# Attention scores over all 128 rows of the array, and the sample's score and sum tiles of four heads in a row

## The chip, the cores and the metric

The kernel runs on one core of a Trainium2 chip. TensorE (PE) multiplies, VectorE (DVE), ScalarE (ACT) and GpSimd (POOL) do the elementwise work, SyncE (SP) issues most of the DMAs. Each engine works through its own list of instructions in order and waits on semaphores for the others. The metric is the device time of one launch in microseconds (us); lower is better.

## The reference

One layer of a streaming encoder, for a prompt of 512 tokens and a sample of 32 tokens that continues a cache of 512. Two branches start from one projection: RWKV-7 time mixing, and differential attention, of which the change touches only the second. Cut to that:

```python
def diff_attend(q, k, v, lam, mask):          # 8 heads, two maps c of 64 dims per head, v of 128 dims
    s = jnp.einsum('bqhcd,bkhcd->bchqk', q, k) * (DA_HEAD_DIM ** -0.5)
    if mask is not None:                       # prompt: block causal, chunks of 64
        s = jnp.where(mask, s, -1e30)
    p = jax.nn.softmax(s, axis=-1)
    pd = p[:, 0] - lam * p[:, 1]
    return jnp.einsum('bhqk,bkhd->bqhd', pd, v)
# sample: keys and values are the 512 cached rows and the 32 new ones, no mask
```

The result is normalised per head and projected (w_o_da), gated together with the other branch, projected again, and goes through a gated feed-forward layer. All of it is float32.

## The kernel before, in words

**Precision.** Most matrix products are done in the format fp32r: every operand is kept as a high part and a low part, and a product is the sum of high x high, high x low and low x high. `dense` (L139 is its matmul) does this for all projections, on weight tiles that `load_w` loads (L119, SP), rounds on ACT (L120) and subtracts on DVE or POOL (L121). The attention's transposes, probability x value products and everything of the sample's attention are plain float32; the trace shows two records for each such matmul.

**Stages.** First the RWKV projections and recurrence (to about 690 us), then the attention of eight heads (690 to 912 us), then merge, output projection, feed-forward and final norm. Under the attention run the *fillers*: the projections of v and of the branch gates that are left over, and the RWKV output projection. They are recorded with a low priority (`tc.high_priority(offset=LOW)`), and a scheduler that plans with its own durations places every engine's instructions: where the attention has nothing ready by its plan, it puts matmuls of L139. The order on each engine is then fixed.

**A head of the prompt** (loop over `h`, L997 on). DMAs of L1008 bring q and k of each map m twice, the 64 dims once on partitions `hi` (the map's own half) and once on `lo` (the other half): `rQ`, `rK`. ACT rounds them to `xQ`, `xK` (L1010). For q, DVE overwrites the `lo` half of `xQ` with the low parts, so `xQ` is [high; low] on 128 rows. For k, `xK` stays high parts on both halves, and the low parts go to the map's half of one tile `KL` (L1012). For each block of 128 queries i and map m, PE does two matmuls into the PSUM tile `sc`:

```python
PE.matmul(sc[m][:, 0:n], Q[m][:, qb], KH[m][:, 0:n], start=True, stop=False)      # L1031: 128 rows
PE.matmul(sc[m][:, 0:n], Q[m][f, qb], KL[f, 0:n], start=False, stop=True)         # L1032: 64 rows
```

DVE takes the row maximum, ACT the exponentials, DVE combines both maps (`pd`), PE transposes `pd` (L1045), ACT copies it (`pdt`), PE multiplies by `vtok` (L1049). Every one of these tiles has few buffers; `rK`, `xK` and `KL` have one.

**The sample** (`attend_sample`, called after heads 3 and 7 for four heads each). For each head e, a DMA brings its 256 KB of cached keys into the one buffer `kc` (L938), and PE does two score matmuls of 64 rows and 32 columns, one a map (L940), at `tile_position=(64 * m, 32 * e)`. L946 does the same for the new keys. After the softmax come, for each head e, a 256 KB DMA of cached values into `vtok` (L987), four matmuls of 128 rows and 32 columns (L989) and one of 32 rows and 32 columns for the new values (L991), at `tile_position=(0, 32 * e)`.

Of the kernel before, what the change touches and what calls it, by code (L numbers as in the profile page):

```python
# [10 lines left out]
F32 = mybir.dt.float32  # L11
F32R = mybir.dt.float32r
# [10 lines left out]
# tiles whose weights are split on GpSimd (projections of the recurrence, as (pair, which)) and on  # L23
# VectorE (the other projections, the recurrence's output projection from 40 on)
# [6 lines left out]
PAST = 512  # L31
# [34 lines left out]
def tile_hybrid_layer(  # L66
# [57 lines left out]
    def dense(src, total, xh, xl, evac, le=None, whole=None):  # L124
        """src: weight tile in DRAM of total row blocks; evac(psum, c0, c1) for both column halves.
        whole: pool that holds all of the tile's weights, for one column half after the other."""
        ps = [psd[0].tile([128, 272], F32, name="psd") for _ in HALVES]
        parts = [(b, min(WK, total - b)) for b in range(0, total, WK)]
        ws = {}
        both = range(len(HALVES))  # L130
        for hf, (base, kt) in ([(h, p) for h in both for p in parts] if whole else [(h, p) for p in parts for h in both]):
            if base not in ws:
                ws[base] = load_w(src[:, base * 128:(base + kt) * 128], kt, le or V, whole or wpool)
            wh, wl = ws[base]
            c0, c1 = HALVES[hf]
            for k in range(kt):
                kk = base + k
                for ip, (w, x) in enumerate(((wh, xh), (wh, xl), (wl, xh))):
                    PE.matmul(ps[hf][:, :c1 - c0], w[:, k, :], x[:, kk, c0:c1],  # L139
                              start=(kk == 0 and ip == 0), stop=(kk == total - 1 and ip == 2))  # L140
            if base + kt == total:
                evac(ps[hf][:, :c1 - c0], c0, c1)
# [5 lines left out]
    def newton_wide(y, x, t):  # L148
        """y ~ x**-0.5, one Newton step, all SBUF"""
        A.activation(out=t, in_=y, func=AF.Square)  # L150
        V.scalar_tensor_tensor(out=t, in0=t, scalar=-0.5, in1=x, op0=ALU.mult, op1=ALU.mult)
        V.scalar_tensor_tensor(out=y, in0=t, scalar=1.5, in1=y, op0=ALU.add, op1=ALU.mult)

    def rsqrt_tiny(pool, x, n, tag):
        """x**-0.5 for a [p, n] tile of positive numbers"""
        p = x.shape[0]
        yt = pool.tile([128, 16], F32, name=tag + "y", bufs=2)
        tt = pool.tile([128, 16], F32, name=tag + "t", bufs=2)
        y, t = yt[:p, :n], tt[:p, :n]
        V.tensor_scalar(out=y.bitcast(I32), in0=x.bitcast(I32), scalar1=-0.5, scalar2=1597463007.0,  # L160
                        op0=ALU.mult, op1=ALU.add)
        for _ in range(4):
            V.tensor_tensor(out=t, in0=y, in1=y, op=ALU.mult)
            V.scalar_tensor_tensor(out=t, in0=t, scalar=-0.5, in1=x, op0=ALU.mult, op1=ALU.mult)
            V.scalar_tensor_tensor(out=y, in0=t, scalar=1.5, in1=y, op0=ALU.add, op1=ALU.mult)
        return y
# [6 lines left out]
    def rms_scale(x, t, rs, ss, c0, c1):  # L173
        """rs[:, c0:c1] <- (ss / 1024 + eps)**-0.5 for the sums of squares ss in PSUM; x, t: scratch"""
# [56 lines left out]
    def shifted(idx, out, rs=None):  # L231
        """evacuation of a projection and the token shift after it; rs: the columns' scale where it is still to come"""
# [32 lines left out]
    # the array's clock rises while the first operands are on their way  # L265
# [45 lines left out]
    # [high; low] parts of both low-rank inputs, for weights held twice  # L311
# [31 lines left out]
    # ================= phase 1: RWKV, q and k projections =================  # L343
# [10 lines left out]
    # persistent work tiles  # L354
# [15 lines left out]
    def diag16(flat):  # L370
        """the two diagonal 16x16 blocks of a 32x32 matrix kept in rows of 32"""
# [5 lines left out]
    def inverse(npf):  # L377
        """diagonal 16-blocks of Xp <- transposed inverses of (I - N) of the strictly lower blocks N of npf"""
# [11 lines left out]
    def rw_rates(p):  # L390
        """decay and in-context rate of a pair's channels"""
# [13 lines left out]
        # decay: tanh of the low-rank product, cumulated in chunks  # L405
# [10 lines left out]
        # in-context rate  # L416
# [4 lines left out]
    def rw_elem(p, Pt, Pi, ta, kr, r, vv):  # L421
# [3 lines left out]
        def head_sum(t, names, use):  # L425
            """use(psum, c0, c1) of t's sums over each head"""
# [9 lines left out]
        # normalised key  # L436
# [16 lines left out]
        # kmod and bonus  # L453
# [11 lines left out]
        # A~ R~ B~ K~, the sample's chunk behind the others  # L465
# [7 lines left out]
        # rows (K; B) of a chunk's products for the even head, (B; K) for the odd one  # L473
# [14 lines left out]
    def chunk_products(dst, m0, a, b):  # L488
        """masked products of a pair's chunks: rows (K; B) for the even head, (B; K) for the odd one"""
# [13 lines left out]
    def join16(rows, src, M, xt):  # L503
        """xt (block diagonal of transposed 16-inverses) <- transposed 32-inverses; src(q, m): transposed N"""
# [23 lines left out]
    def rw_super(s):  # L528
# [3 lines left out]
        # inverses of the 16-blocks of every chunk, then of the 32-blocks, then the block below them  # L532
        # (even heads have their rows at partitions 64.., odd heads at 0..)
# [38 lines left out]
    def rw_chain(p0, ms):  # L572
# [19 lines left out]
        # chain over the chunks  # L592
# [52 lines left out]
    def rw_norm(p0, ysb):  # L645
        """group norm over the head's values, bonus, gate"""
# [28 lines left out]
    def by_dims(d):  # L675
        """rows of all heads' maps as [map, dim, token]; a tile of a projection holds 8 dims of every map"""
        return d.rearrange("a (m d) t -> (a m) d t", m=2)
# [137 lines left out]
    # rotary on the staged rotated halves  # L815
# [38 lines left out]
    # ================= attention =================  # L854
# [10 lines left out]
    lamp = ap.tile([128, 2, 64], F32, name="lamp")  # L865
    lamv = ap.tile([128, 4, 64], F32, name="lamv")
# [10 lines left out]
    def attend_norm(po, rz0, n):  # L877
        """po [128, n, 128] unnormalised outputs, rz0 [128, n]: returns normalised SBUF tile"""
# [24 lines left out]
    def put_z(ps, hs, c0, c1):  # L903
        """the normalised outputs of heads hs in PSUM, scaled and split"""
# [21 lines left out]

    def attend_sample(g):
# [7 lines left out]
        kc, vc = {}, {}  # L935
        for e, hh in enumerate(hs):
            kc[e] = ap.tile([128, PAST], F32, name="kc")
            nc.sync.dma_start(out=kc[e], in_=kcache[hh])  # L938
            for m in range(2):
                PE.matmul(sc[m][32 * e:32 * e + 32, :], qks[m * 64:m * 64 + 64, 0, hh, :],  # L940
                          kc[e][m * 64:m * 64 + 64, :], start=True, stop=True,
                          tile_position=(64 * m, 32 * e))
        scn = [misc() for _ in range(2)]
# [40 lines left out]
        for e, hh in enumerate(hs):  # L984
            q = slice(32 * e, 32 * e + 32)
            vc[e] = ap.tile([128, 4, 128], F32, name="vtok", bufs=3)
            nc.sync.dma_start(out=vc[e], in_=vcache[hh])  # L987
            for b in range(4):
                PE.matmul(po[q, 0, :], pdt[:, b, q], vc[e][:, b, :], start=(b == 0), stop=False,  # L989
                          tile_position=(0, 32 * e))  # L990
            PE.matmul(po[q, 0, :], pdtn[:, q], vs[:, e, :], start=False, stop=True, tile_position=(0, 32 * e))  # L991
# [5 lines left out]
    for h in range(HEADS):  # L997
        vt = ap.tile([128, TOK], F32, name="vt")
        nc.sync.dma_start(out=vt, in_=v_d[h])
        # every map's q as [high; low] parts, k's high parts twice, k's low parts  # L1000
        Q, KH = [], []
        KL = ap.tile([128, TOK], F32R, name="KL")
        for m in range(2):
            hi, lo = slice(m * 64, m * 64 + 64), slice(64 - m * 64, 128 - m * 64)
            for t, (d, n) in enumerate(((q_d, "Q"), (k_d, "K"))):
                raw = ap.tile([128, TOK], F32, name=f"r{n}{m}")
# [4 lines left out]
                o, f = (x, lo) if t == 0 else (KL, hi)  # L1011
                V.tensor_tensor(out=o[f, :], in0=raw[f, :], in1=x[f, :].bitcast(F32), op=ALU.subtract)  # L1012
                (KH if t else Q).append(x)
        vtok = ap.tile([128, 4, 128], F32, name="vtok", bufs=3)
# [6 lines left out]
        for i in range(4):  # L1021
# [5 lines left out]
            for m in range(2):  # L1027
                f, qb = slice(m * 64, m * 64 + 64), slice(i * 128, (i + 1) * 128)
                # never under 256 columns: fewer take longer
                n = max(nk, 256)  # L1030
                PE.matmul(sc[m][:, 0:n], Q[m][:, qb], KH[m][:, 0:n], start=True, stop=False)  # L1031
                PE.matmul(sc[m][:, 0:n], Q[m][f, qb], KL[f, 0:n], start=False, stop=True)  # L1032
# [28 lines left out]
    # ================= merge =================  # L1061
# [15 lines left out]
    # ================= output projection, residual =================  # L1077
# [32 lines left out]
    # ================= FFN =================  # L1110
# [5 lines left out]
    with tc.tile_pool(name="up", bufs=1) as up:  # L1116
# [3 lines left out]
        # what the stored rows and the bias add to those two tokens  # L1120
# [7 lines left out]
        for f in range(FT):  # L1128
            cc = []
            for i in range(2):  # L1130
# [13 lines left out]
                # the sample's first two tokens follow the stored state  # L1144
# [195 lines left out]
```

## Time and profile before

| | us |
|---|---|
| median of three timed runs | 1410.44 (1406.54 to 1412.62) |
| span of the profiled execution | 1413.8 |
| of it the attention, 690 to 912 us | 222 |
| PE busy over the span | 1327.3 (94%) |

Of the profiled execution only the span is given, from its first to its last instruction; it is 3.4 us above the median of the timed runs. A busy PE in the page is not a PE at its peak: matmuls overlap, and a record's duration is longer than the distance to the next record's start. The distances between starts tell what a matmul costs its successors.

### The profile page before, as it was taken

Reading aid. Unit: us, or ns where it says so; the run is one execution under the profiler, and the core shown is the slowest. Engines: PE = TensorE matmul, PEld = TensorE weight load, DVE = VectorE, ACT = ScalarE, POOL = GpSimd, SP = SyncE. Lnnn points to the kernel's source line nnn. Section 1 sums busy time; section 2 is a strip of 40 time slices with the busy share of each in tenths; the row PEclk is TensorE's granted clock in tenths of the full one; section 3 lists DMA queues with packets and bytes.
Section 4 is the critical chain, followed back from the end, with each engine's and each line's share of the span. In section 5 each row is a group of like instructions: output and inputs, shape, how many; then the busy total and the mean of one; then the engine's idle time right before and its main releaser. Section 6 shows DMA issues by size and latency. Waiting matters only on the chain. (4 is left out here: it accounts for less than half of the span.)

```text
span 1413.8 us, 29892 instructions
## 1 busy us (share of the span) xinstructions
PE 1327.3 (94%) x12014; PEld 1217.9 (86%) x12014; DVE 904.1 (64%) x1881; ACT 590.8 (42%) x1222; POOL 229.3 (16%) x262
## 2 busy tenths in 40 slices
PE   7799996899987799999999999999999999999997
PEld 7799896787777687788887787899999999999996
DVE  6777789555668424355478586566787788774333
ACT  5577643444212133132377455333544444443220
POOL 6601202001123100122132111000111111111111
PEclk9899997799999699999999999999999999999999
DMA  5356561333476134332566432246322222235321
GB/s 168 95 174 183 160 216 62 108 111 114 133 231 207 41 101 142 95 123 79 163 199 209 151 112 83 77 144 189 110 89 84 90 88 85 90 98 152 104 81 64
DMA packets 122217, 176.96 MB, mean 125 GB/s; under 512 B 40032, under 2 KB 47072, under 8 KB 122080
## 3 DMA queue, kind: packets, MB, share of 16 engines
q1 hardware_dynamic: 108720, 153.81, 35.6%
q10 hardware_dynamic: 13360, 21.26, 4.3%
q8 instruction: 94, 1.54, 0.4%
q14 instruction: 43, 0.35, 0.1%
HBM read 137.34 MB, written 37.41 MB: 124 GB/s over the span
## 5 line engine op out<-in xcount | busy, mean ns | idle before, releaser
L120 ACT CAST wh<-wr 128x512 fp32r<-128x512 f32 (+1 forms) x316 | 193.1, 614 | 395.7 <-PE psd L139 327.1
L139 PE MATMUL psd<-h_h,wl 128*128 128x272 f32 x976 | 298.6, 306 | 3.4 <-POOL wl L121 2.4
L139 PE MATMUL psd<-h_h,wh 128*128 128x272 f32 x976 | 299.5, 307 | 0.7 <-ACT qt L687 0.7
L139 PE MATMUL psd<-h_l,wh 128*128 128x272 f32 x976 | 298.0, 305 | 0.2 <-DVE h_l L334 0.2
L121 DVE TENSOR_TENSOR wl<-wr,wh 128x512 fp32r<-128x512 f32 x230 | 156.3, 683 | 100.5 <-ACT wh L120 94.9
L139 PE MATMUL psd<-xgh,wl 128*128 128x272 f32 x704 | 204.2, 290 | 0.0
L139 PE MATMUL psd<-xgl,wh 128*128 128x272 f32 x704 | 203.6, 289 | 0.0
L139 PE MATMUL psd<-xgh,wh 128*128 128x272 f32 x704 | 202.5, 288 | 0.0
L139 PEld LDWEIGHTS psd<-h_h,wl 128*128 128x128 f32 x976 | 192.5, 197 | 9.7 <-issue 2.8
L139 PEld LDWEIGHTS psd<-h_h,wh 128*128 128x128 f32 x976 | 192.9, 198 | 8.1 <-issue 3.5
L139 PEld LDWEIGHTS psd<-h_l,wh 128*128 128x128 f32 x976 | 192.8, 198 | 7.9 <-issue 3.1
L121 POOL TENSOR_TENSOR wl<-wr,wh 128x512 fp32r<-128x512 f32 x86 | 120.4, 1404 | 427.8 <-ACT wh L120 299.4
L139 PEld LDWEIGHTS psd<-xgl,wh 128*128 128x128 f32 x704 | 132.9, 189 | 0.0
L139 PEld LDWEIGHTS psd<-xgh,wl 128*128 128x128 f32 x704 | 132.7, 188 | 0.0
L139 PEld LDWEIGHTS psd<-xgh,wh 128*128 128x128 f32 x704 | 132.3, 188 | 0.1
L139 PE MATMUL psd<-ah,wh 128*128 128x272 f32 x352 | 101.9, 289 | 0.0
L139 PE MATMUL psd<-al,wh 128*128 128x272 f32 x352 | 101.6, 289 | 0.0
L139 PE MATMUL psd<-ah,wl 128*128 128x272 f32 x352 | 101.5, 288 | 0.0
L139 PE MATMUL psd<-mh,wl 128*128 128x272 f32 x256 | 76.4, 298 | 0.0
L139 PE MATMUL psd<-ml,wh 128*128 128x272 f32 x256 | 75.3, 294 | 0.0
L139 PE MATMUL psd<-mh,wh 128*128 128x272 f32 x256 | 74.9, 292 | 0.0
L1138 POOL COPY cvo<-uf 128x2 f32<-128x2 f32 x88 | 37.1, 452 | 220.5 <-DVE uf L1135 220.5
(390 smaller groups left out, 2674.2 us busy)
## 6 DMA issues: line engine op xcount, KB each, us to landing
wr<-w_in SPq DMA_DIRECT2D x132, 256.0 KB, 3.4
wr<-w_up SPq DMA_DIRECT2D x88, 256.0 KB, 2.8
wr<-w_down SPq DMA_DIRECT2D x40, 256.0 KB, 2.7
arL<-ar_d SPq DMA_DIRECT2D x16, 512.0 KB, 5.0
bkL<-bk_d SPq DMA_DIRECT2D x16, 512.0 KB, 3.8
ar_d<-ar SPq DMA_DIRECT2D x8, 544.0 KB, 4.1
t_d<-qt ACTq DMA_DIRECT2D x16, 272.0 KB, 2.6
rQ<-q_d SPq DMA_DIRECT2D x32, 136.0 KB, 3.1
```

The lines of the kernel that those rows point to most:

```text
L120: A.copy(out=wh[:, :n], in_=raw)
L121: le.tensor_tensor(out=wl[:, :n], in0=raw, in1=wh[:, :n].bitcast(F32), op=ALU.subtract)
L139: PE.matmul(ps[hf][:, :c1 - c0], w[:, k, :], x[:, kk, c0:c1], start=(kk == 0 and ip == 0), stop=(kk == total - 1 and ip == 2))
L1138: G.tensor_copy(out=cvo[:, t, :, w], in_=u[:, 512 + w::32])
```

## The change

The low parts of the keys are subtracted for both halves and stay in place in `rK`, which is then an fp32r tile of 128 rows: `KL` becomes one such tile a map, and the second score matmul takes all 128 rows. It adds low x low to the sum. For the sample, the keys of four heads are one DMA of 1 MB (`load_caches`, issued at heads 0 and 4, ahead of that head's own loads) into `kc`, and the values of four heads another one into the same single buffer, issued once the scores are recorded. The sum matmuls run with the block b outside and the head e inside, and the four matmuls for the new values follow them. `vtok` goes from three buffers to two, and two small tiles for lambda take buffers of `pd`. The rest of the diff blanks comments.

```diff
+    def load_caches(g):
+        caches[g] = ap.tile([128, 4, PAST], F32, name="kc")
+        nc.sync.dma_start(out=caches[g], in_=kcache[4 * g:4 * g + 4].rearrange("a p t -> p a t"))
...
-        kc, vc = {}, {}
+        kc = caches[g]
         for e, hh in enumerate(hs):
-            kc[e] = ap.tile([128, PAST], F32, name="kc")
-            nc.sync.dma_start(out=kc[e], in_=kcache[hh])
             for m in range(2):
                 PE.matmul(sc[m][32 * e:32 * e + 32, :], qks[m * 64:m * 64 + 64, 0, hh, :],
-                          kc[e][m * 64:m * 64 + 64, :], start=True, stop=True,
+                          kc[m * 64:m * 64 + 64, e, :], start=True, stop=True,
                           tile_position=(64 * m, 32 * e))
+        vc = ap.tile([128, 4, PAST], F32, name="kc").rearrange("p a (b v) -> p a b v", v=128)
+        nc.sync.dma_start(out=vc, in_=vcache[4 * g:4 * g + 4].rearrange("a p b v -> p a b v"))
...
-        for e, hh in enumerate(hs):
-            q = slice(32 * e, 32 * e + 32)
-            vc[e] = ap.tile([128, 4, 128], F32, name="vtok", bufs=3)
-            nc.sync.dma_start(out=vc[e], in_=vcache[hh])
-            for b in range(4):
-                PE.matmul(po[q, 0, :], pdt[:, b, q], vc[e][:, b, :], start=(b == 0), stop=False,
+        Q4 = [slice(32 * e, 32 * e + 32) for e in range(4)]
+        for b in range(4):
+            for e, q in enumerate(Q4):
+                PE.matmul(po[q, 0, :], pdt[:, b, q], vc[:, e, b, :], start=(b == 0), stop=False,
                           tile_position=(0, 32 * e))
+        for e, q in enumerate(Q4):
             PE.matmul(po[q, 0, :], pdtn[:, q], vs[:, e, :], start=False, stop=True, tile_position=(0, 32 * e))
...
+        if h % 4 == 0:
+            load_caches(h // 4)
...
-                raw = ap.tile([128, TOK], F32, name=f"r{n}{m}")
+                kept = ap.tile([128, TOK], F32R if t else F32, name=f"r{n}{m}")
+                raw = kept.bitcast(F32) if t else kept
...
-                o, f = (x, lo) if t == 0 else (KL, hi)
-                V.tensor_tensor(out=o[f, :], in0=raw[f, :], in1=x[f, :].bitcast(F32), op=ALU.subtract)
-                (KH if t else Q).append(x)
-        vtok = ap.tile([128, 4, 128], F32, name="vtok", bufs=3)
+                if t == 0:
+                    V.tensor_tensor(out=x[lo, :], in0=raw[lo, :], in1=x[lo, :].bitcast(F32), op=ALU.subtract)
+                    Q.append(x)
+                else:
+                    V.tensor_tensor(out=kept, in0=raw, in1=x.bitcast(F32), op=ALU.subtract)
+                    KH.append(x)
+                    KL.append(kept)
+        vtok = ap.tile([128, 4, 128], F32, name="vtok", bufs=2)
...
-                PE.matmul(sc[m][:, 0:n], Q[m][f, qb], KL[f, 0:n], start=False, stop=True)
+                PE.matmul(sc[m][:, 0:n], Q[m][:, qb], KL[m][:, 0:n], start=False, stop=True)
```

The scheduler plans the attention anew, so rows move on all engines from there on. On PE, at the sums of the first four heads of the sample, before (L980 transposes the small probabilities, L1031 and L1032 are the next head's scores, L139 fillers):

```order
L980 MATMUL tp_9857<-cst_92,pdn_9847 32x128
L1031 MATMUL sc1_9976<-xK1_9939,xQ1_9933 128x256
L1032 MATMUL sc1_9976<-KL_9917,xQ1_9933 128x256
L139 MATMUL psd_8569<-mh_8533,wh_8571 128x272
L139 MATMUL psd_8569<-ml_8534,wh_8571 128x272
L139 MATMUL psd_8569<-mh_8533,wl_8570 128x272
L989 MATMUL po_9861<-vtok_9862,pdt_9855 32x128 x4
L991 MATMUL po_9861<-vs_9792,pdtn_9859 32x128
L989 MATMUL po_9861<-vtok_9869,pdt_9855 32x128 x4
L991 MATMUL po_9861<-vs_9792,pdtn_9859 32x128
L989 MATMUL po_9861<-vtok_9876,pdt_9855 32x128 x4
L991 MATMUL po_9861<-vs_9792,pdtn_9859 32x128
```

The fourth head's two rows stand 22 rows further down. The same place now (L986 is that transpose, L993 and L996 are the sums, L1042 and L1043 the prompt's scores):

```order
L986 MATMUL tp_9849<-cst_92,pdn_9839 32x128
L139 MATMUL psd_8633<-mh_8533,wh_8636 128x272
L139 MATMUL psd_8633<-ml_8534,wh_8636 128x272
L139 MATMUL psd_8633<-mh_8533,wl_8635 128x272
L139 MATMUL psd_8634<-mh_8533,wh_8636 128x272
L139 MATMUL psd_8634<-ml_8534,wh_8636 128x272
L993 MATMUL po_9853<-kc_9807,pdt_9847 32x128 x16
L996 MATMUL po_9853<-vs_9790,pdtn_9851 32x128 x4
L1042 MATMUL sc0_9986<-xK0_9912,xQ0_9906 128x384
L1043 MATMUL sc0_9986<-rK0_9909,xQ0_9906 128x384
```

Sixteen sum matmuls stand in a row, then the four for the new values; before, the two kinds alternated head by head.

On SP, at the loads of q and k of the third head, before (wr are the fillers' weights; the brackets name whom the row waits for):

```order
L119 DMA wr_8172<-w_in 128x512 [waits DMAHW6_49,Pool_49]
L119 DMA wr_8208<-w_in 128x512 [waits DMAHW7_49,Pool_49]
L1008 DMA rQ0_9445<-q_d_66 64x544 [waits DMAHW0_49,DVE_49]
L1008 DMA rQ0_9445<-q_d_66 64x544 [waits DMAHW1_49]
L1008 DMA rK0_9451<-k_d_69 64x544 [waits DMAHW2_49,DVE_49]
L1008 DMA rK0_9451<-k_d_69 64x544 [waits DMAHW3_49]
```

And now (zr and mg are the other branch's tiles, vt is the head's v):

```order
L119 DMA wr_8370<-w_in 128x512 [waits DMAHW7_49,DMAHW5_49,Pool_49]
L119 DMA wr_8406<-w_in 128x512 [waits DMAHW1_49,DMAHW0_49,Pool_49]
L914 DMA mg_7870<-t_d_68 128x544 [waits DMAHW5_49]
L1015 DMA rK0_9450<-k_d_69 64x544 [waits DMAHW2_49,PE_49]
L1006 DMA vt_9442<-v_d_67 128x544 [waits DMAHW3_49,PE_49]
L1015 DMA rK0_9450<-k_d_69 64x544 [waits DMAHW4_49]
L1015 DMA rQ0_9618<-q_d_66 64x544 [waits DVE_49,Activation_49]
```

The load of k waited for DVE's subtraction of the head before; it now waits for PE, for the last score matmul of the head before, which still reads `rK`, and it stands behind more weight loads.

## Rows read from the trace of the kernel before

**Rows 1.** The page, part 1: busy us, share and instructions of each engine.

```profile
PE 1327.3 (94%) x12014; PEld 1217.9 (86%) x12014; DVE 904.1 (64%) x1881; ACT 590.8 (42%) x1222; POOL 229.3 (16%) x262
```

**Rows 2.** Windows: us, then busy PE, PEld, DVE, ACT, POOL, granted clock, DMA.

```profile
690.00:912.00 222.00, 218.37 (x1461) 177.98 (x1460) 147.62 (x480) 125.96 (x363) 39.97 (x28) 1.00 0.48 146
912.00:1386.00 474.00, 474.00 (x3765) 473.28 (x3764) 312.72 (x593) 191.28 (x304) 51.37 (x102) 1.00 0.34 107
```

**Rows 3.** Timeline of PE, one 64-row matmul: start us, duration us, engine, line, operands.

```profile
698.75 0.28 PE L139 MATMUL psd<-h_h,wh 128*128 128x272 f32 x1
698.87 0.28 PE L139 MATMUL psd<-h_l,wh 128*128 128x272 f32 x1
699.08 0.38 PE L1032 MATMUL sc<-KL,xQ 64*128 64x256 f32 x1
699.39 0.40 PE L139 MATMUL psd<-h_h,wl 128*128 128x272 f32 x1
699.62 0.29 PE L139 MATMUL psd<-h_h,wh 128*128 128x272 f32 x1
```

**Rows 4.** Waits of PE, 690 to 912 us: us in total, times, longest.

```profile
PE psd L139 <- POOL wl L121: 0.9, 1, 0.9
PE psd L139 <- DVE mg L917: 0.9, 1, 0.9
```

**Rows 5.** Timeline of PE, two visits of the sample's score matmuls.

```profile
767.89 1.04 PE L940 MATMUL sc<-kc,qks 64*32 64x512 f32 x2
...
784.70 0.28 PE L139 MATMUL psd<-h_l,wh 128*128 128x272 f32 x1
784.91 1.05 PE L940 MATMUL sc<-kc,qks 64*32 64x512 f32 x4
785.89 0.39 PE L139 MATMUL psd<-h_h,wl 128*128 128x272 f32 x1
786.12 0.29 PE L139 MATMUL psd<-h_h,wh 128*128 128x272 f32 x1
```

**Rows 6.** Timeline of PE, the new keys' scores of four heads and one map.

```profile
789.46 0.27 PE L946 MATMUL tp<-qks 64*32 64x32 f32 x8
```

**Rows 7.** Timeline of PE, the sample's sums of heads 4 to 7.

```profile
898.02 1.06 PE L989 MATMUL po<-vtok,pdt 128*32 128x128 f32 x8
899.01 0.40 PE L991 MATMUL po<-vs,pdtn 32*32 32x128 f32 x2
899.35 1.06 PE L989 MATMUL po<-vtok,pdt 128*32 128x128 f32 x8
...
901.99 0.39 PE L139 MATMUL psd<-ml,wh 128*128 128x272 f32 x1
...
904.53 0.29 PE L139 MATMUL psd<-dh,wl 128*128 128x272 f32 x1
904.75 1.06 PE L989 MATMUL po<-vtok,pdt 128*32 128x128 f32 x8
905.74 0.40 PE L991 MATMUL po<-vs,pdtn 32*32 32x128 f32 x2
906.07 0.40 PE L139 MATMUL psd<-dh,wh 128*128 128x272 f32 x1
906.31 0.29 PE L139 MATMUL psd<-dl,wh 128*128 128x272 f32 x1
```

**Rows 8.** Instructions of tile rK: durations ns min/median/max, and DMA landing.

```profile
L1008 SPq DMA_DIRECT2D rK<-k_d x32: 444/587/1450, 690.9 to 839.6; - x32
L1010 ACT CAST xK<-rK x16: 633/646/652, 696.8 to 849.9; 128x544 fp32r<-128x544 f32 x16
DMA to landing us min/median/max: 2.5/3.2/4.8
```

**Rows 9.** The page, part 6: a 512 KB load, us to landing.

```profile
arL<-ar_d SPq DMA_DIRECT2D x16, 512.0 KB, 5.0
```

**Rows 10.** Waits of SP's queue, 680 to 915 us: total us, times, longest.

```profile
SPq L119 <- POOL wl L121: 38.1, 10, 9.1
```

More of the change, by code (lines that the diff above doesn't have):

```diff
@@ L863, in misc @@
         return pst.tile([128, 512], F32, name="tp")
-    lamp = ap.tile([128, 2, 64], F32, name="lamp")
-    lamv = ap.tile([128, 4, 64], F32, name="lamv")
+    lamp = ap.tile([128, 512], F32, name="pd", bufs=2)[:, 0:128].rearrange("p (a b) -> p a b", a=2)
+    lamv = ap.tile([128, 512], F32, name="pd", bufs=2)[:, 0:256].rearrange("p (a b) -> p a b", a=4)
     nc.sync.dma_start(out=lamv.rearrange("p a b -> p (a b)"), in_=params[:, NPAR - 256:NPAR])
@@ L925, in tile_hybrid_layer @@
     nc.sync.dma_start(out=vsc, in_=v_d[:, :, SOFF:TOK].rearrange("a p t -> p a t"))
+    caches = {}
+    def load_caches(g):
+        caches[g] = ap.tile([128, 4, PAST], F32, name="kc")
+        nc.sync.dma_start(out=caches[g], in_=kcache[4 * g:4 * g + 4].rearrange("a p t -> p a t"))
     def attend_sample(g):
@@ L997, in tile_hybrid_layer @@
     for h in range(HEADS):
+        if h % 4 == 0:
+            load_caches(h // 4)
         vt = ap.tile([128, TOK], F32, name="vt")
         nc.sync.dma_start(out=vt, in_=v_d[h])
-        Q, KH = [], []
-        KL = ap.tile([128, TOK], F32R, name="KL")
+        Q, KH, KL = [], [], []
         for m in range(2):
@@ L1027, in tile_hybrid_layer @@
             for m in range(2):
-                f, qb = slice(m * 64, m * 64 + 64), slice(i * 128, (i + 1) * 128)
+                qb = slice(i * 128, (i + 1) * 128)
                 n = max(nk, 256)
                 PE.matmul(sc[m][:, 0:n], Q[m][:, qb], KH[m][:, 0:n], start=True, stop=False)
-                PE.matmul(sc[m][:, 0:n], Q[m][f, qb], KL[f, 0:n], start=False, stop=True)
+                PE.matmul(sc[m][:, 0:n], Q[m][:, qb], KL[m][:, 0:n], start=False, stop=True)
                 V.memset(sc[m][0:64, nk - 64:nk], -1e30)
```

## Prediction

> **What bounds the kernel now.** I read the page's busy shares first: PE is busy 94% of the span and no other engine above 64% [rows 1]. The windows then show where this is tight. In the attention, 690 to 912 us, PE is busy 218.4 of 222 us at full clock (2.4 GHz), with DVE at 147.6 (66%), ACT at 126.0 (57%) and POOL at 40.0; in the 474 us behind it PE has no idle time at all [rows 2]. So the end is set by PE's list: a microsecond less of PE's time in the attention, if PE does not stand still instead, ends the kernel a microsecond earlier, because what follows is a closed row of matmuls that only moves up. The waits of PE in that stage that name another engine are short, two of 0.9 us at the head of the list [rows 4].
>
> Busy time does not tell what PE's time consists of, so the timeline comes next, by the distance from start to start. A filler of 272 columns takes 0.12 us (698.75 to 698.87), which I round to 0.125. Around a 64-row score matmul of 256 columns the distances are 0.21, 0.31 and 0.23 us (698.87 to 699.62), 0.75 us for three matmuls that at this rate take 0.37 [rows 3]. The array loses 0.38 us when its shape changes from 128x128 to 64x128 and back. Shapes of 64x32, 128x32 and 32x32 behave alike: score matmuls of the sample begin 0.21 us behind the filler ahead of them, and the second filler behind them is 0.23 us late [rows 5].
>
> **Part by part: the prompt's scores.** There are 64 low-part matmuls (8 heads, 4 blocks, 2 maps), and in PE's order before they make 63 separate changes of shape (two stand side by side once). The change makes all of them 128x128, as the high-part matmul is already; columns and count stay. Removed: 63 x 0.38 = 23.9 us of PE. DVE's subtraction works on 128 partitions instead of 64 with the same 544 columns; I take it at nothing, since DVE has a third of the stage free [rows 2].
>
> **The sample's scores.** A visit costs 784.70 to 786.12 less two fillers, 1.42 - 0.25 = 1.17 us, with both maps of a head side by side (x4, two records a matmul), and as long with one map (x2, 1.04 us) [rows 5]. Before, there are 10 visits (five for each four heads: the single `kc` buffer makes each head wait for its DMA); now there are 5 (four heads' tiles of one map together, three times, and one map split into 1 and 3). If four column tiles run as side by side as the two row tiles do, this removes 5 x 1.17 = 5.9 us. That they do is seen only on small tiles: eight records of four heads, two each, are over in 0.27 us [rows 6].
>
> **The sample's sums.** A head takes 898.02 to 899.35, 1.33 us, because the 32-row matmul behind its four 128-row ones changes the shape; three heads take 3.97 us (898.02 to 901.99) and the fourth, alone, 904.53 to 906.31 less two fillers, 1.53 us [rows 7]. With 0.2 us for the first three's entry and exit (1.53 - 1.33), four heads cost 3.97 + 0.2 + 1.53 = 5.7 us. Now one change to 128x32 holds sixteen matmuls and one to 32x32 holds four; side by side they take what the lone head takes, 1.53 us, and say 0.1 us for the more numerous issues. Removed: 2 x (5.7 - 1.6) = 8.2 us.
>
> The trace of before has no long tiles in four column groups. The ends are full overlap as above, and none, which is a rival below. The Trainium skill, TensorE: Matmul & The Clock Gate, Part 3, gives 2.38 times for three column tiles of 512 columns rather than 3; at that ratio four tiles take 1.26 times one, and five score and two sum visits would give back about 2 us. The eight records in 0.27 us [rows 6] show overlap and not its ratio; my sum takes full overlap.
>
> **What it adds: k is loaded later.** `rK` now holds the low parts until the head's last score matmul, so the next head's k on that map cannot be fetched ahead. Behind that matmul (about 0.4 us to its end, its columns and the tail of a record) come two DMA issues on SP (0.59 us each, the second runs from there), its landing (3.2 us), and ACT's cast (0.65 us): 0.4 + 0.59 + 3.2 + 0.65 = 4.8 us, from 4.1 at the shortest landing to 6.4 at the longest [rows 8]. Behind the first score matmul of the next head all of PE's list waits; behind the waiting load on SP stand the head's v, the q of the head after and the next fillers' weights, which PE needs later. What covers this is PE's own work between the two: in the new order the tightest place (heads 5 to 6, map 0) has 22 fillers, three matmuls of 512 columns and eight transposes, 22 x 0.125 + 3 x 0.235 + 8 x 0.12 = 4.4 us, the others up to 5.9 us; heads 3 to 4 have over 20 us. So six transitions are tight. At the median landing they lack 0.4 us or nothing, together about 1 us; at the longest landing, 0.5 to 2 us each, about 9 us. I take 3 us, near the median, since SP and ACT are seldom free at once.
>
> **The 1 MB loads.** Each has 1 MB in one DMA; 512 KB land in 5.0 us [rows 9], so 1 MB is bounded by some 3.2 us (a small load) and 10 us (twice that). The values have the softmax and over 100 rows of PE as cover, the keys of heads 4 to 7 three heads; these cost nothing. Exposed are what queues behind: q, k and v of head 0, ahead of which the new order puts 25 more fillers (3.1 us), and k of head 5, which is issued some 3 us behind the second key load. Between 0 and 6 us; I take 2, as the fillers cover half.
>
> **Waits that come closer.** PE does the stage's 222 us in about 184 then, and DVE's share rises to 147.6 / 184 = 80%. Waits that were just met are then missed. Nothing in the trace prices this; the nearest rows are the two waits of 0.9 us [rows 4]. Between 0 and 10 us, I take 3. A gain is excluded for these three terms, since none takes work from PE.
>
> **Sum.** 23.9 + 5.9 + 8.2 = 38.0 us removed, 3 + 2 + 3 = 8 us given back: 30 us less. The profiled span of 1413.8 us becomes 1384; it lies 3.4 us above the median of the timed runs, 1410.4, which becomes 1380.4.
>
> **Rivals.** *Column tiles run one after another.* A score tile's two passes take about 0.9 us of a visit's 1.05 [rows 5]; the 16 tiles take 16 x 0.9 and the five changes of shape 5 x 0.27, 15.8 us instead of 10 x 1.17 = 11.7, and the sums save only the three changes of shape between the heads, some 0.2 us each, 1.2 us in both groups. Then 23.9 - 4.1 + 1.2 - 8 = 13.0 us less, 1397. Against it stand the eight records in 0.27 us [rows 6].
>
> *The load of k is held up in SP's queue.* SP issues in order, and in the new order the load of k stands behind fillers' weights that wait for POOL; such waits were 3.8 us in the mean (38.1 in 10) and 9.1 at most [rows 10]. If half of the mean falls on each tight transition, 6 x 1.9 = 11 us go, 19 us less, 1391. This ends *slower than before* if the hold is the longest one: 6 x 9.1 = 55 us against 30, 1435. It decides from 5 us a transition on top of the 4.8 us. Against it: the planner put the weight loads ahead because it expects them sooner, and POOL is busy only 40 of 222 us [rows 2].
>
> *The gain is used up.* If PE waits for ACT and DVE at each of the 32 query blocks as it ran ahead of them, 32 x 0.9 us [rows 4] = 29 us go, and the time stays within 0.5%. For it speaks only that no row shows these engines at the higher pace; against it their idle third.
>
> **How the numbers follow.** Forecast (23 to 42 us less, 1368 to 1387): 0.62. Held up in SP's queue or more waits, 10 to 23 us less: 0.2. Column tiles serial: 0.07. Used up: 0.06. Slower: 0.05. The range leaves out used up, slower, half of the serial case, and a little at the low end where even the 8 us don't come: 1368 to 1397. A measurement of this kernel can tell about 0.5%, 7 us, from no change. Faster by more: 0.62 + 0.2 + 0.07 = 0.89; the same 0.06; slower 0.05.
>
> **What the changed profile would show.** Right: fillers 0.125 us apart on both sides of every prompt score; four column tiles of 512 columns over in about 1.05 us, and the sixteen sum matmuls in about 1.1; the attention some 30 us shorter with the 474 us behind it unchanged. Wrong: score visits of 3 us or more; PE waiting for ACT's `xK` or for a DMA at the first score of each head by more than 1 us; SP's waits for POOL just ahead of the loads of k; gaps of PE before transposes and value products that name ACT or DVE.

## The result, and the profile after

The changed kernel takes 1394.08 us in the median (1390.51 to 1395.73), the kernel before beside it 1411.37. The ratio is 0.9871, 95% interval 0.9844 to 0.9898: 17.3 us less, beyond the 0.5% that can be told. The forecast was 1380.4, 30 us less, with a range of 1368 to 1397. The time lies in the range, and little more than half of the forecast gain arrived.

The page of the changed kernel, part 1, against [rows 1]: the span is 1388.4 us, and PE is busy 33 us less; the other engines are where they were.

```profile
PE 1294.1 (93%) x12014; PEld 1204.7 (87%) x12014; DVE 903.1 (65%) x1881; ACT 590.2 (43%) x1222; POOL 230.0 (17%) x262
```

Windows of the attention and of the stretch behind it (us; then busy PE, PEld, DVE, ACT, POOL, granted clock, DMA), against [rows 2]: behind the attention PE is closed as before. In the attention it now has 14 us of 205 in which it does nothing; before it had 4 of 222.

```profile
690.00:895.00 205.00, 190.64 (x1478) 171.65 (x1477) 152.82 (x492) 128.09 (x367) 38.72 (x27) 1.00 0.52 159
895.00:1361.00 466.00, 466.00 (x3707) 465.45 (x3706) 306.12 (x578) 187.84 (x296) 51.99 (x102) 1.00 0.34 105
```

Timeline of PE round a low-part matmul (start us, duration us, engine, line, operands), against [rows 3]: 128 rows, and every start 0.12 to 0.13 us behind the last. The change of shape is gone.

```profile
698.67 0.29 PE L139 MATMUL psd<-h_h,wl 128*128 128x272 f32 x1
698.79 0.28 PE L1043 MATMUL sc<-rK,xQ 128*128 128x256 f32 x1
698.91 0.29 PE L139 MATMUL psd<-h_h,wh 128*128 128x272 f32 x1
```

The same view of a visit of the sample's scores and of the sums of four heads, against [rows 5, 7]: four heads' score tiles (eight records) take 1.06 us, as one head's did, and twenty sum matmuls of four heads 1.36 us (793.50 to 794.86), as the lone head's five did (904.75 to 906.07, 1.32).

```profile
764.74 1.06 PE L944 MATMUL sc<-kc,qks 64*32 64x512 f32 x8
765.73 0.40 PE L139 MATMUL psd<-h_h,wh 128*128 128x272 f32 x1
...
793.50 1.08 PE L993 MATMUL po<-kc,pdt 128*32 128x128 f32 x32
794.51 0.42 PE L996 MATMUL po<-vs,pdtn 32*32 32x128 f32 x8
794.86 0.44 PE L1042 MATMUL sc<-xK,xQ 128*128 128x384 f32 x1
```

Waits of PE (us in total, times, longest), against [rows 4]: this list is new. It names the softmax's chain, link by link: the exponential that must have read the scores before the next block's scores may be written (L1046), the difference of the two maps (`pd`), the normalised output (`on`). One row names the late low parts (`rK`), one the head's v.

```profile
PE sc L1042 <- ACT E L1046: 3.6, 4, 1.5
PE tp L1064 <- DVE on L886: 2.3, 5, 0.8
PE tp L1056 <- DVE pd L1052: 1.5, 3, 0.7
PE sc L944 <- ACT E L1046: 1.1, 2, 0.6
PE tp L999 <- DVE rz L1048: 1.0, 1, 1.0
PE tp L1028 <- DMA vt<-v_d: 0.8, 1, 0.8
PE tp L1056 <- DVE dl L906: 0.8, 1, 0.8
...
PE sc L1043 <- DVE rK L1022: 0.6, 1, 0.6
```

**One balance for all kernels.** From the last matmul of the recurrence's gate (`psg`) to the first sum of the second norm, PE executes the same 2,239 records in every kernel, 1,641 of them fillers (in the second kernel with three score tiles it is seven fillers more). A transpose is one record here and a value product two. The stretch is taken apart by the distances from start to start. A record at the full-array pace costs 0.109 us (128 columns), 0.119 (256), 0.125 (272), 0.172 (384) or 0.222 (512); that is 260.7 us in each kernel (0.9 more with the seven fillers). What is above falls into four columns: visits of 64-row matmuls beyond their own columns, up to the second start behind them; visits of the sample's small tiles; waits of over 0.15 us; shorter gaps (a stretch at half clock lands there).

| kernel | stretch, us | 64-row visits | sample's visits | waits | short gaps |
|---|---|---|---|---|---|
| before | 322.8 | 26.5 (63) | 24.9 | 4.8 (10) | 5.9 |
| after | 302.1 | 0 | 11.9 | 18.4 (31) | 11.1 |

So 26.5 + 13.0 us were removed, and waits and gaps gave back 13.6 + 5.2: 20.7 us remain. The rest of the 25.4 us between the two spans lies outside, 4.2 of it ahead, in the recurrence, which is the same in both; there the granted clock stands at its lower level (1.2 GHz) for 92 us now and stood there for 103 before. The two profiled executions are further apart than the medians, by 8 us: the span before, 1413.8, is above the four timed runs beside the change, and the changed kernel's profile is that of the shortest of its four. Of the 18.4 us, 14.3 name a link of the softmax's chain, 1.1 the late k, 1.0 v, 2.0 the fillers' weights and outputs.

### The profile page after: what moved, and what is told of

Its sections match the earlier page's. It is cut to its first block, busy times and chain, and to the rows that moved or that the text cites. A ratio compares the mean times of both kernels' runs of the same rounds, so it can differ in the third digit from the quotient of the medians.

```text
span 1388.4 us, 29891 instructions
## 1 busy us (share of the span) xinstructions
PE 1294.1 (93%) x12014; PEld 1204.7 (87%) x12014; DVE 903.1 (65%) x1881; ACT 590.2 (43%) x1222; POOL 230.0 (17%) x262
## 5 line engine op out<-in xcount | busy, mean ns | idle before, releaser
L139 PE MATMUL psd<-h_h,wh 128*128 128x272 f32 x976 | 298.2, 306 | 3.3 <-ACT qt L687 3.3
L139 PE MATMUL psd<-h_h,wl 128*128 128x272 f32 x976 | 296.6, 304 | 3.8 <-POOL wl L121 2.7
L139 PE MATMUL psd<-h_l,wh 128*128 128x272 f32 x976 | 296.6, 304 | 0.2 <-DVE h_l L334 0.2
L139 PE MATMUL psd<-xgh,wl 128*128 128x272 f32 x704 | 204.1, 290 | 0.0
L139 PE MATMUL psd<-xgh,wh 128*128 128x272 f32 x704 | 203.1, 289 | 0.0
L139 PE MATMUL psd<-xgl,wh 128*128 128x272 f32 x704 | 202.3, 287 | 0.0
L139 PEld LDWEIGHTS psd<-h_h,wh 128*128 128x128 f32 x976 | 192.2, 197 | 9.3 <-ACT qt L687 3.8
L139 PEld LDWEIGHTS psd<-h_h,wl 128*128 128x128 f32 x976 | 191.7, 196 | 8.9 <-POOL wl L121 3.2
L139 PEld LDWEIGHTS psd<-h_l,wh 128*128 128x128 f32 x976 | 192.1, 197 | 5.6 <-issue 1.2
L139 PEld LDWEIGHTS psd<-xgl,wh 128*128 128x128 f32 x704 | 132.7, 189 | 0.0
L139 PEld LDWEIGHTS psd<-xgh,wl 128*128 128x128 f32 x704 | 132.4, 188 | 0.0
L139 PEld LDWEIGHTS psd<-xgh,wh 128*128 128x128 f32 x704 | 132.3, 188 | 0.1
L139 PE MATMUL psd<-ah,wh 128*128 128x272 f32 x352 | 101.8, 289 | 0.0
L139 PE MATMUL psd<-ah,wl 128*128 128x272 f32 x352 | 101.5, 288 | 0.0
L139 PE MATMUL psd<-al,wh 128*128 128x272 f32 x352 | 101.5, 288 | 0.0
L139 PE MATMUL psd<-mh,wl 128*128 128x272 f32 x256 | 74.7, 292 | 0.0
L139 PE MATMUL psd<-ml,wh 128*128 128x272 f32 x256 | 74.2, 290 | 0.0
L139 PE MATMUL psd<-mh,wh 128*128 128x272 f32 x256 | 74.2, 290 | 0.0
```

## The experiments

Three theories. **Pace:** PE has lost its slow places, and the chain from scores to values, as long as ever, is now late at many points of PE's fixed list. **Late loads:** k in place and the 1 MB loads make PE wait. **Size:** the changes of shape cost less than was taken. Each kernel is given with its ratio to the kernel before on the same chip and its row of the balance. The last column is no part of the sum: it is the time in the stretch, from the granted clock, at the lower clock level (before 6.1 us, after 3.4). The diffs show only the lines that matter.

| kernel | median us, ratio (95%) | stretch | 64-row visits | sample's | waits | short gaps | at lower clock |
|---|---|---|---|---|---|---|---|
| after, 64 rows | 1405.9, 0.9937 (0.9917 to 0.9958) | 311.4 | 25.5 (60) | 10.6 | 8.1 (20) | 6.5 | 3.4 |
| before, 128 rows | 1402.9, 0.9924 (0.9895 to 0.9953) | 313.7 | 0 | 25.7 | 16.1 (33) | 11.2 | 6.0 |
| prompt's part | 1404.8, 0.9938 (0.9918 to 0.9958) | 314.3 | 0 | 27.7 | 15.8 (26) | 10.1 | 3.4 |
| sample's part | 1410.4, 0.9985 (0.9964 to 1.0006) | 323.1 | 27.7 (63) | 9.4 | 16.0 (24) | 9.2 | 16.0 |
| control | 1394.3, 0.9870 (0.9841 to 0.9898) | 306.2 | 0 | 11.9 | 21.1 (35) | 12.5 | 9.7 |
| k ahead | 1407.2, 0.9948 (0.9922 to 0.9975) | 318.8 | 0 | 14.7 | 27.4 (40) | 16.0 | 23.9 |
| three score tiles | 1399.2, 0.9922 (0.9896 to 0.9948) | 307.5 | 0 | 10.9 | 21.9 (43) | 14.1 | 15.7 |
| the same, attention only | 1400.1, 0.9905 (0.9868 to 0.9942) | 310.5 | 0 | 8.8 | 27.5 (41) | 12.7 | 20.2 |
| casts on GpSimd | 1407.2, 0.9972 (0.9950 to 0.9993) | 317.0 | 0 | 11.4 | 30.9 (40) | 14.0 | 12.6 |
| no maximum | 1397.4, 0.9903 (0.9862 to 0.9943) | 311.2 | 0 | 10.9 | 26.5 (33) | 13.1 | 16.6 |
| key load behind | 1398.0, 0.9902 (0.9869 to 0.9934) | 307.7 | 0 | 9.9 | 23.9 (33) | 13.2 | 12.8 |

At the lower level a filler starts 0.22 to 0.23 us behind the last and not 0.125, so about half of the last column is lost at most (an estimate). That bears on every comparison below: in the changed kernel it is 1.7 us, in the others up to 12, and a part of what stands under waits, visits and gaps is the clock's. It is the same 3.4 us in the changed kernel and in the one with 64 rows.

**The changed kernel with 64 rows again.**

```diff
-PE.matmul(sc[m][:, 0:n], Q[m][:, qb], KL[m][:, 0:n], start=False, stop=True)
+PE.matmul(sc[m][:, 0:n], Q[m][m * 64:m * 64 + 64, qb], KL[m][m * 64:m * 64 + 64, 0:n], start=False, stop=True)
```

> The changed kernel with one thing back: the low-part matmul reads 64 rows again (its map's half of the 128-row tiles; the products are the same). The order on every engine is that of the changed kernel. 64 matmuls change the array's shape again. Pace theory (38 us were removed, and some 18 us came back as waits of TensorE for ScalarE and VectorE because it ran ahead of them): TensorE needs 63 x 0.38 = 24 us more, but 8 to 12 us of these fall into waits that are there anyway, so 1394 + 12 to 16 = 1406 to 1410, with waits of over 0.15 us between the first value transposes and the last transposes of outputs falling from 16 us to some 6. Late-load theory (waits stand because k and the 1 MB loads land late, and they end at a fixed time after a matmul of TensorE's own): the waits stay and the whole 24 us come on top, 1418. Size theory (the change of shape costs less than 0.38 us): 1394 + 10 or less, under 1404, with the distances around the 64-row matmuls shorter than in the kernel before.

1405.9, at the lower edge of the pace theory's range; by the ratios, which leave the chips' difference out, it is 9.3 us above the changed kernel, and by that alone the size theory (10 or less) would also stand. This is the cleanest comparison of the study, since no instruction changes its place. The distances decide: the changes of shape cost 25.5 us here, so the size theory falls. The stretch grows by 9.3 us only, because 10.3 us of waits, 4.6 of short gaps and 1.2 at the sample's visits are gone. PE's waits in this kernel, the rows that answer to those above:

```profile
PE tp L1056 <- DVE pd L1052: 1.0, 3, 0.4
PE sc L1042 <- ACT E L1046: 0.9, 1, 0.9
PE tp L1064 <- DVE on L886: 0.8, 2, 0.5
PE tp L1028 <- DMA vt<-v_d: 0.6, 1, 0.6
```

One place in both timelines, the changed kernel first and then the one with 64 rows. In the first PE stands 0.77 us for the exponential; in the second the same score matmul starts 0.40 us behind the same filler instead of 1.06.

```profile
741.04 0.29 PE L139 MATMUL psd<-h_h,wl 128*128 128x272 f32 x1
742.10 0.44 PE L1042 MATMUL sc<-xK,xQ 128*128 128x384 f32 x1 [0.77 <-ACT E L1046]
742.38 0.34 PE L1043 MATMUL sc<-rK,xQ 128*128 128x384 f32 x1
```

```profile
748.30 0.29 PE L139 MATMUL psd<-h_h,wl 128*128 128x272 f32 x1
748.70 0.44 PE L1042 MATMUL sc<-xK,xQ 128*128 128x384 f32 x1
749.07 0.44 PE L1043 MATMUL sc<-rK,xQ 64*128 64x384 f32 x1
749.43 0.39 PE L139 MATMUL psd<-h_h,wh 128*128 128x272 f32 x1
749.66 0.29 PE L139 MATMUL psd<-h_l,wh 128*128 128x272 f32 x1
```

**The kernel before with 128 rows, and the prompt's part alone.** The first changes one line of the kernel before; the second takes over from the change all that concerns `Q`, `KH`, `KL`.

```diff
-PE.matmul(sc[m][:, 0:n], Q[m][f, qb], KL[f, 0:n], start=False, stop=True)
+PE.matmul(sc[m][:, 0:n], Q[m][:, qb], KL[:, 0:n], start=False, stop=True)
```

> The kernel before, its low-part matmul over all 128 rows of the same shared low-part tile, so that each map's scores also take in products with the other map's low parts (that part of the computation is wrong). No tile, load or sum is changed, only the shape. If 63 changes of shape at 0.38 us are the price and nothing else is late: 1411 - 24 = 1387. Pace theory: some of it comes back as waits for ScalarE and VectorE, here with neither k later nor 1 MB loads: 1411 - 24 + 4 to 10 = 1391 to 1397, and the waits name ScalarE's exponentials and VectorE. Late-load theory: the give-back in the changed kernel comes from its loads, which are not here, so 1387 to 1389. Size theory: 1400 or more.

> The prompt's part of the change alone: the low parts of k over 128 rows, kept in the tiles the loads land in, the sample as before. By the prediction's terms: 24 removed, 3 for k loaded later, some 2 for waits that come closer: 1411 - 19 = 1392. Pace theory: 24 removed and 8 to 10 back, 1395 to 1397. Late-load theory: k's load is most of the give-back, 10 or more, 1397 or above, with TensorE waiting for ScalarE's cast of k or VectorE's low parts at first scores of a head.

They gain 10.6 and 8.7 us by the medians. By the numbers alone the first would speak for the size theory (1400 or more) and the second for late loads (1397 or above). The balance tells otherwise: all 26.5 us of 64-row visits are gone, and 16.6 us (128 rows) and 15.2 us (prompt's part) of them come back as waits and short gaps. The first has neither k in place nor a 1 MB load, so the give-back needs neither (its list of PE was planned anew as well, from the first low-part matmul on). In the second, the rows that name the cast of k or its low parts sum to 3.0 us, not to 10. The waits of the first name the same links and, in its shared tile, the low parts:

```profile
PE sc L1032 <- DVE KL L1012: 2.4, 4, 1.1
PE sc L1031 <- ACT E L1035: 2.4, 5, 0.9
PE tp L1045 <- DVE pd L1041: 1.9, 4, 0.6
```

The medians of the two, without k in place and with it, are 1.9 us apart, inside their scatter.

**The sample's part alone.** All of the change that concerns `caches`, `vc`, `Q4` and the order of sums; the prompt's lines as before. The recurrence's outputs land in rows of the gate's tile:

```diff
-zr = pool.tile([128, TOK], F32, name="zr", bufs=2)
+zr = mg[:, 6 + k % 2, :]
```

> The sample's part of the change alone: 1 MB loads of the cached keys and values, score tiles and sums of four heads side by side, the prompt's scores as before (k loaded ahead, 64-row low parts). To make room the eight loads of the recurrence's outputs land in two rows of the tile for the gate, loaded later, instead of in two tiles of their own. By the prediction's terms: 5.9 + 8.2 = 14.1 removed, 2 for the loads: 1411 - 12 = 1399. Pace theory: TensorE is at a lower pace than in the changed kernel and few waits are added, 1397 to 1400. Late-load theory with the 1 MB loads at fault: 6 us or more back, 1403 or above. Size theory (column tiles overlap less than fully): 1405 or above.

The time hardly moves: 1410.4, where the late-load and the size theory had put it. Yet the visits fall from 24.9 to 9.4 us, more than the prediction's terms say, so it is not the size: 14.5 us come back in waits and gaps, and the 64-row visits take 1.2 us more. The largest rows are one wait at the output projection's start (`mg`) and the chain's end (`on`):

```profile
PE tp L1060 <- DVE on L886: 3.4, 3, 1.6
PE psd L139 <- DVE mg L917: 3.3, 1, 3.3
PE psd L139 <- ACT qt L687: 1.4, 1, 1.4
```

No row names a 1 MB load. Nor is this the pace theory's number (1397 to 1400), though the rows name its links: PE's list was drawn up anew, and in the new list PE meets waits that the old one didn't have, at 64-row pace. The clock has a share too: 16.0 us at the lower level against 6.1 before, an estimated 5 us lost at most. How much of the rest is the list and how much the pace, this run does not tell.

**K ahead, with its control.** The control has the landing place above in the changed kernel; the other one in addition has tiles of their own for the low parts.

```diff
-V.tensor_tensor(out=kept, in0=raw, in1=x.bitcast(F32), op=ALU.subtract)
+V.tensor_tensor(out=KL[m], in0=raw, in1=x.bitcast(F32), op=ALU.subtract)
```

> A control for the next kernel. The changed kernel, in which the eight loads of the recurrence's outputs land in two rows of the gate's tile (loaded later) instead of in two tiles of their own; this gives back 4.25 KB a partition, and the work is the same. Every theory: 1394, within 5, and the stretch from the last matmul of the recurrence's gate to the first sum of the second norm 302 us, within 4.

> As the control, but the low parts of k go into tiles of their own, so that the next head's k is fetched ahead as in the kernel before; the matmuls stay 128 rows. Late-load theory (k that lands late is most of the 13.6 us of added waits): the waits of TensorE fall from 18 us to 8 or less, 1394 - 10 = 1384 or below. Pace theory (TensorE runs ahead of the softmax's chain): only the rows that name the low parts or the cast of k go, 1 to 2 us, and the others stay; within 3 us of the control, 1391 to 1397.

The control holds in the timed runs (1394.3); its stretch of 306.2 us is just outside the 302 ± 4. Its list of PE is that of the changed kernel, place by place, so the two rows of the balance show what two profiled executions of one list differ by: 4.1 us, with one wait, for the first head's v, of 3.8 us instead of 1.0 and the clock at its lower level for 7 us from within that wait on. Smaller differences between rows of the table tell little.

K fetched ahead makes the kernel slower: 1407.2, single runs from 1397.0 to 1411.5, the profiled one at the upper end. The late-load theory wanted 1384, the pace theory 1391 to 1397; both are missed. One row still names the late low parts (`KL`, 0.8 us; `rK` in the control, 0.6), one for a late q is new (`xQ`, 1.1), and the waits of the chain have grown. Of the 16.7 us by which the stretch is longer than the changed kernel's, up to 10 are the clock's:

```profile
PE tp L1063 <- DVE on L886: 4.5, 4, 1.7
PE tp L1055 <- DVE pd L1051: 4.2, 7, 1.2
PE sc L1041 <- ACT E L1045: 2.6, 4, 1.8
```

**Three score tiles in turn.** Two versions; the second has the fillers' third PSUM tile back behind the attention.

```diff
-sc = [pssc.tile([128, 512], F32, name=f"sc{m}") for m in range(2)]
+sc = [pssc.tile([128, 512], F32, name="sc", bufs=3) for m in range(2)]
```

> The changed kernel with three PSUM tiles in turn for the scores of both maps instead of one for each map; the PSUM bank comes from the fillers' (two instead of three). A score matmul no longer has to wait until ScalarE's exponentials have read the last block's scores of the same map. Pace theory: the waits of first scores for ScalarE (4.6 + 0.6 us at the prompt's, 1.4 at the sample's) go, and a part comes back at the transposes behind: 1394 - 3 to 6 = 1388 to 1391. Late-load theory: no change, 1394, or slower by the fillers' fewer tiles.

> Three PSUM tiles in turn for the prompt's and the sample's scores as in the earlier run with three, but the fillers have two PSUM tiles only in the attention and three again behind it (with two, the stretch behind the attention took 414.4 instead of 408.9 us). Pace theory: waits for the exponentials are gone (0.5 us there) while those of the next links and of k's cast (3.6 us) and low parts (2.1 us) have taken their place, so the 5 us of the tail come back and nothing else: 1399 - 5 = 1394, within 4. If the fillers' fewer tiles were what cost time in the attention itself as well, 1397 or more.

The time is 1399.2, not 1388 to 1391. Taken one by one the foreseen waits went: the first scores wait 0.5 us for exponentials instead of 4.6. The sum did not follow. Others took the place, in the first version:

```profile
PE sc L1042 <- ACT xK L1017: 4.3, 5, 1.7
...
PE tp L1056 <- DVE pd L1052: 2.4, 4, 1.0
PE psd L139 <- ACT qt L687: 2.1, 2, 1.1
PE tp L1064 <- DVE on L886: 1.9, 4, 0.9
```

Behind the stretch the second version takes 409.5 us again (the first 414.4), but its stretch is 3 us longer; 1400.1 is above my 1394 ± 4. The clock can account for 6 us of the first stretch and 8 of the second (half of what the last column has above the changed kernel's 3.4), and they are 5 and 8 us longer than the changed kernel's.

**The casts of q and k on GpSimd.**

```diff
-A.copy(out=x, in_=raw)
+G.tensor_copy(out=x, in_=raw)
```

> The changed kernel with the casts of q and k (32 of 0.65 us, 21 us of ScalarE) on GpSimd. If ScalarE's queue makes the exponentials late (one form of the pace theory), the waits that name ScalarE (about 8 of 18 us) go: 1386 to 1390. If it is the length of the chain itself (scores, maximum, exponential, difference, transposes), which the casts seldom delay: 1392 to 1396. Late-load theory: GpSimd's cast takes longer than 0.65 us, so k is later still at six transitions, and the time goes up by 3 to 10 us, 1397 to 1404.

1407.2, above every number given. ScalarE has 18 us less to do in the stretch, and PE waits longer for its exponentials, 5.7 us in 5 against 3.6 in 4, and for `on`, 5.8. ScalarE itself now stands 26.3 us for VectorE's maxima (`nm`) instead of 11.0. So in this list a relieved ScalarE does not deliver earlier; it waits for the link ahead of it. The test is not clean: VectorE, which has that link, is itself busy 219.6 us of the stretch instead of 209.1, and the order is another.

**No maximum.**

```diff
...
-V.tensor_reduce(out=nm[:, m:m + 1], in_=sc[m][:, 0:nk], axis=AX.X, op=ALU.max, negate=True)
-A.activation(out=E[:, m, 0:nk], in_=sc[m][:, 0:nk], func=AF.Exp, bias=nm[:, m:m + 1], scale=1.0,
+A.activation(out=E[:, m, 0:nk], in_=sc[m][:, 0:nk], func=AF.Exp, scale=1.0,
...
```

> The changed kernel without the maximum in the prompt's softmax: the 64 reductions of the scores on VectorE (30.2 us of it, 0.48 us each) are left out and the exponentials take the scores as they are, so the chain from scores to values is a link shorter and VectorE is busy some 120 instead of 149 us of the stage. The order is planned anew with the shorter chain. Pace theory in the form that VectorE and ScalarE are too busy at the new pace: the added waits go, 18 us to 6 or less, 1394 - 12 = 1382 or below. Pace theory in the form that each wait is a link later than the order allows, however busy the engines are: the order moves the transposes up as the chain gets shorter, and the waits stay within 4 us of 18; 1390 to 1396. Late-load theory: the waits for k and v stay and are met more often, 1394 to 1400.

1397.4, near the second form of the pace theory and inside the late-load theory's 1394 to 1400; its waits are 26.5 us, not within 4 of 18. VectorE is busy 182.5 us of the stretch instead of 209.1 and the chain is a link shorter, but PE's waits for links of the chain sum to 14.8 us, against 14.3 in the changed kernel; the rest is mainly v and the output projection's start:

```profile
PE sc L1041 <- ACT E L1044: 4.6, 5, 1.8
PE tp L1062 <- DVE on L886: 4.2, 3, 2.6
PE tp L1028 <- DMA vt<-v_d: 4.1, 1, 4.1
```

With 13% of VectorE's work gone the chain's waits are the same, which speaks against VectorE's load as their cause. It does not settle it, since the list was drawn up for the shorter chain. The clock has up to 6.6 of the 9.1 us by which the stretch is longer.

**The key load behind the head's own loads.** `load_caches` moved below q and k.

> The changed kernel with the 1 MB load of the cached keys issued behind v, q and k of the head at which it stands (heads 0 and 4) instead of ahead of them. Late-load theory with the 1 MB loads: the waits of the value transposes for v (1.0 us in the changed kernel's profile, 3.8 in the control's) go, 1394 - 1 to 4 = 1390 to 1393. Pace theory: the same on that point, and everything else stays: 1390 to 1394.

PE does not wait for v any more, so the 1 MB load was what delayed it (1.0 us in the changed kernel; 3.8, 4.3 and 4.3 in the control, in the kernel without maximum and in the second with three tiles): the first head's v lands 3.9 us after its issue in the kernel before and 3.7 here, but 8.9 to 10.4 in those four. But the list is another, first scores wait 4.1 us for k's cast, and the time is 1398.0, above both forecasts.

## Why the prediction was half right

**What was removed** was sized well. The shape: 23.9 us forecast, 26.5 measured, 0.42 us a visit and not 0.38. I had priced one visit, of 256 columns. Its last part, 0.1 us between the two records behind it, is 0.2 where the first of them is again a score, and some visits have a short wait in them. The Trainium skill, TensorEngine Tiling (Array Packing), Key Properties, says that a change of tiling mode drains the array; it gives no price, and the trace of before gives 0.42 us in the mean for there and back. The sample's scores: 5.9 forecast, 6.0 (from 12.0 to 5.9 with waits out of the way, in the kernel with 64 rows). The sums: 8.2 forecast, 8.2 (11.4 to 3.1, rounded). Together, rounded, 40.8 instead of 38.0. The serial rival is dead: four tiles take one tile's time. The ratio of 2.38 for three column tiles (the Trainium skill, TensorE: Matmul & The Clock Gate, Part 3), which the prediction set beside its sum, does not show here: 1.06 us for four against 1.04 for one.

**What was given back** was 20 us in the two profiles, and not 8; by the medians, 17.3 us less, it would be 3 more. K loaded later: 3 forecast, 1.1 in the rows that name it, 3.0 in those of the prompt's part alone, and 1.9 between the two medians above; the rival with SP's queue did not come, though SP waits for POOL as before (35.3 us in 13 waits, 38.1 in 10 before). The 1 MB loads: 2 forecast, 1.0 here, 3.8 with the same list in the control and about 4 in other lists. **The step that failed is "waits that come closer": 3 us taken, 10 the upper bound, about 18 measured** (40.8 - 20.7, less the 2 us for k and v). I bounded it by two waits of 0.9 us in the trace of before. But those rows came from a kernel in which PE lost 0.42 us at each low-part matmul, that is, 63 times just behind the scores whose exponentials PE has to wait for. The loss was the cover. The right row to look at was the distance in PE's list from a score to the transposes that need its result, priced without the loss; no run here tried that bound.

The rival "the gain is used up" had this mechanism, at 29 us, and I gave it 0.06 because ACT and DVE had an idle third. An idle third says nothing about a chain: each link waits for the one ahead of it, so its engines can idle while PE waits for them. The changed kernel has both: VectorE is idle for 52 of the attention's 205 us, and yet PE waits 14.3 us for the chain.

**What is shown and what is not.** Shown, with one and the same order: with the shape's loss back, the stretch grows by 9.3 us only, and 16 of the 25.5 us vanish, 10.3 of them in waits that were there and 4.6 in short gaps. Shown: k and the 1 MB loads are not needed for it. Not shown: why each list places its steps as it does; no trace tells what durations the planner took. Nor why the sample's part alone brings waits at the old pace. No version beat the changed kernel: all six that took away one suspected wait had more waiting in sum and took 1397 to 1407 us. Only two of them, k ahead and the casts on GpSimd, are slower than the changed kernel beyond both intervals, and of the longer stretches 5 to 10 us can be the clock's. Among the kernels with both parts and 128 rows the waits go from 18 to 31 us, and the changed kernel has the fewest.

## To carry to other kernels

When a loss is removed from the busiest engine, look at what stands in its list within a few microseconds behind each place where the loss sat: waits that the loss covered appear there, and they may take half of the gain. My advice, untried here: bound them by the distance from each producer to its consumer at the new pace, not by the waits in the old trace, and don't read an idle share of the other engines as room. An edit that changes an automatic order is two edits; only a pair with the same order, such as the one with 64 rows, gives a clean price.

## Of the hardware, not expected

Four column tiles of 64 x 32, each with 512 columns, run wholly side by side: 1.06 us, against 1.05 for a head's two row tiles and 1.04 for a single tile [rows 5].

A wait can cost more than its length. In the kernel with k ahead PE stood still for 1.3 of the 4 us up to 769 and for 0.7 of the next 2, most of it one wait of 1.83 us for an exponential, and the granted clock fell from its upper level (2.4 GHz) to 0.50, the lower (1.2 GHz). It stayed there 12 us although PE was busy throughout; at half pace these are some 6 us lost. Windows of that kernel:

```profile
765.00:769.00 4.00, 2.71 (x18) 2.19 (x17) 3.99 (x7) 2.05 (x6) 3.24 (x3) 1.00 0.61 199
769.00:771.00 2.00, 1.27 (x6) 1.18 (x7) 1.99 (x10) 1.99 (x6) 0.00 (x0) 0.83 0.57 155
771.00:783.00 12.00, 12.00 (x44) 6.19 (x44) 5.57 (x12) 4.78 (x11) 1.56 (x2) 0.50 0.48 125
783.00:787.00 4.00, 4.00 (x30) 3.81 (x30) 3.85 (x3) 2.30 (x5) 2.60 (x2) 0.88 0.98 260
```

The changed kernel's clock is 1.00 through its attention: its 31 waits, none over 1.7 us, did not set it off. Nor did it fall there in the kernel before, in the one with 64 rows, in the kernel before with 128 rows or in the prompt's part. In each of the other eight it fell at least once, for 3 to 14 us, mostly within or just behind a wait of 1.3 to 4.1 us: such a wait was paid twice.
